# Early loads on one queue, position tables begun ahead, and a re-cut end of the last product and norm

## The chip, the cores and the metric

The kernel runs on one core of one Trainium2 chip. The metric is device time in microseconds (us) of one execution, from launch to the last output byte. Engines are named as the profile names them: PE (TensorE matrix products), PEld (its weight loads), DVE (VectorE), ACT (ScalarE), POOL (GpSimd) and SP (SyncE, used here to issue DMAs). Each engine works through its own instructions in order; engines wait for each other and for DMAs by semaphores.

## The reference

A decoder trunk of four pre-norm residual layers over one sequence of 256 tokens, width 1024, float32:

```python
cos, sin = rope_tables(positions)
h = x
for i in range(4):
    a = rms_norm(h, attn_norm_g[i])
    y = (diff_attention, moba_attention, swa_sink_attention)[i % 3](a, ...)   # w_in, heads, w_out
    h = h + y
    a = rms_norm(h, mlp_norm_g[i])
    h = h + square(maximum(a @ w_up[i], 0)) @ w_down[i]
return rms_norm(h, final_norm_g)
```

`rope_tables` turns the 256 integer positions into 8 cosines and 8 sines each, used by every mixer on the first 16 of each head's 64 dimensions. The differential attention of layers 0 and 3 also needs a number lambda from four short vectors. All weights, 183 + 2 pieces of 1 MB, are read from memory once.

## The kernel before

**Layout.** The residual stream lies transposed in four tiles `hT[j]`, each with two blocks `d` of 128 features by 256 tokens. Float32 products are made from three passes of a rounded format: each operand is split into a high and a low part, and `mm3` (lines 275 to 277) adds hi·hi, hi·lo and lo·hi in PSUM. A matmul of 128 x 128 by 128 x 512 is the unit.

**Weights.** `fetch` loads 1 MB pieces with DMAs issued from SP, into 4 buffers `raw`. `stage` rounds a piece on ACT into `whi` (line 80) and takes the rest on DVE into `wlo` (line 81), with 3 buffers of each. `take` hands out a piece, fetching 5 ahead and staging 2 ahead.

**Start.** Before any product there are: loads of `x` (by `load_x`: the first two blocks, the gains `gn` and the positions `posi` from ACT, the rest from SP between the pieces of the first two weight tiles, which come in quarters of 256 KB); 10 warm-up products on a tile of ones (20 PE instructions, line 134); staging of two pieces; and `norm_part` for each block `d`, which makes the high part of gain times `x` on ACT (line 232, tile `hg`) and the low part on DVE (line 233). `norm_sum` squares and adds (lines 237 to 246); `norm_factor` ends in `rsqrt`, whose result `nr` is applied when a product leaves PSUM.

**First layer.** `mixer_layer` makes six products `p_in` by `proj`, in the order q/k 0, q/k 1, v, q/k 2, q/k 3, v. After the first it emits `rotary_tables` (lines 156 to 192: some 37 DVE instructions of 16 elements in a chain, then two Sin on ACT, which need a table load) and `lambdas` (lines 195 to 206: a load `lv` from SP, DVE work, an Exp with its table load). `rope` (lines 306 to 311) then turns q and k, and the step `QK` transposes them on PE (`p_qk`, line 461).

**Order.** The code is written in the order of priority. A planner, which has its own estimate of times, sets the order in which each engine gets its instructions; that order is fixed when the program is built. PE too: in the trace `p_qk` stands behind 104 products `p_in`, though the code has it after 72.

**End.** `down_out` makes the last product, `p_last`, for two column halves `c` of 512 and two token halves `t` of 128. Eight weight pieces `q` with four blocks `k` each go into each half `c`. Each `c` ends with an update of the residual `res` on DVE (line 705), a sum of squares on ACT (line 707), and after the second half, for each `t`, the final norm: lines 712 and 713, `rsqrt` with 1 + 3 x 3 instructions on one column, a scaling of one half on ACT (line 716) and of the other on DVE (line 718), and two output DMAs.

Of the kernel before, what the change touches and what calls it, by code (L numbers as in the profile page):

```python
# [18 lines left out]
P = 128  # L19
D = 1024  # L20
# [9 lines left out]
FAR = 5  # L30
WARM = 10
RAW = 4
# [6 lines left out]
@with_exitstack  # L39
def trunk(ctx: ExitStack, tc: tile.TileContext, xT, positions, gains, lams, swa_row, fng, weights, out):  # L40
    nc = tc.nc
# [16 lines left out]

    def fetch(between=None):
        i = len(fetched)  # L60
        raw = sb.tile([P, 2048], F32, tag="raw", name=f"raw{i}", bufs=RAW)
        if between is None:
            nc.sync.dma_start(raw, weights[i])
        else:
            for h in range(4):
                s = slice(h * 512, (h + 1) * 512)
                nc.sync.dma_start(raw[:, s], weights[i, :, s])
                if h % 2:
                    between()
        fetched.append(raw)  # L70

    def stage():
        i = len(staged)
        raw = fetched[i]
        hi = sb.tile([P, 2048], F32R, tag="whi", name=f"whi{i}", bufs=LOOK + 1)
        lo = sb.tile([P, 2048], F32R, tag="wlo", name=f"wlo{i}", bufs=LOOK + 1)
        w = 512 if i < 2 else 1024
        for h in range(2048 // w):
            s = slice(h * w, (h + 1) * w)
            A.activation(hi[:, s], raw[:, s], AF.Copy)  # L80
            V.tensor_tensor(lo[:, s], raw[:, s], f(hi[:, s]), op=OP.subtract)  # L81
        staged.append((hi, lo))
# [12 lines left out]
    def r3(n):  # L95
        return lambda t: t.rearrange("p (a b) -> p a b", a=n)
# [3 lines left out]
    xv = xT.rearrange("(b p) t -> p b t", p=P)  # L100
    gn = cst.tile([P, 2 * DEPTH * 8 + 2], F32, name="gn")
    gv = gn[:, :2 * DEPTH * 8].rearrange("p (k l b) -> p k l b", k=2, l=DEPTH)
    posi = cst.tile([P, NT], I32, name="posi")
    loaded = []

    def load_x():
        j = len(loaded)
        if j == 0:
            nc.scalar.dma_start(hT[0][:, :S], xv[:, 0, :])
            nc.scalar.dma_start(gn, gains)  # L110
            nc.scalar.dma_start(hT[0][:, S:], xv[:, 1, :])
            nc.scalar.dma_start(posi, positions)
        elif j < 4:
            nc.sync.dma_start(r3(2)(hT[j]), xv[:, 2 * j:2 * j + 2, :])
        loaded.append(j)

    first_act = cst.tile([P, 1], F32, name="first_act")
    V.memset(first_act, 0.0)
    load_x()
# [8 lines left out]
    make_identity(nc, ident)  # L128
    ones = cst.tile([P, P], F32, name="ones")
    G.memset(ones, 1.0)  # L130

    warm = bank("wk", "p_warm")
# [18 lines left out]
    nlam = cst.tile([P, 2], F32, name="nlam")  # L151
    sg = gn[:, 2 * DEPTH * 8:]

    def rotary_tables():

        posf = cst.tile([P, NT], F32, name="posf")
        V.tensor_copy(posf, posi)
        inv = np.float32(THETA) ** (-np.arange(0, 16, 2, dtype=np.float32) / np.float32(16))
        invt = cst.tile([P, NT, 8], F32, name="invt")
        for j in range(8):  # L160
            G.memset(invt[:, :, j:j + 1], float(inv[j]))
        an = cst.tile([P, NT, 8], F32, name="an")
# [45 lines left out]
    def rsqrt(y, x, n):  # L208

        t = tiny.tile([P, n], F32, tag="nw", name="nw", bufs=5)  # L210
# [68 lines left out]
    def proj(n, widths, ahead=False, midway=()):  # L279
# [10 lines left out]
        steps = [(t, k) for t in range(NT) for k in range(8)]  # L290
        for t, k in sorted(steps, key=lambda x: x[1]) if ahead else steps:
            if (t, k) == (1, 0):
                for do in midway:
                    do()
            hi, lo = (r3(kb)(x)[:, k % kb, :] for x in parts[k // kb])
            s = slice(P * t, P * t + P)
            x = n.both[k // 2][:, k % 2]
            mm3(out[t], x[:, 0, s], x[:, 1, s], hi, lo,
                k == 0 and (t == 0 or width == 512 or not ahead), k == 7, skip_group_check=True)
        return out  # L300
# [179 lines left out]
    def mixer_layer(i, n):  # L480
# [46 lines left out]
        else:  # L527
# [32 lines left out]
            def OUT(g):  # L560
                if mixer == 0:
                    parts.extend(next(pairs[g]))

            order = (0, 1, "v", 2, 3, "v")
            plan = [[], [], [(QK, 0), (SC, 0)], [(SC, 1)], [(TR, 0), (QK, 1), (SC, 2)], [(TR, 1), (SC, 3)],
                    [(TR, 2), (AV, 0)], [(TR, 3), (AV, 1)], [(AV, 2), (QK, 2), (OUT, 0), (SC, 4)], [(AV, 3), (SC, 5)],
                    [(TR, 4), (QK, 3), (OUT, 1), (SC, 6)], [(TR, 5), (SC, 7)],
                    [(AV, 4), (TR, 6), (AV, 5), (TR, 7), (AV, 6), (OUT, 2), (AV, 7), (OUT, 3)]]
# [117 lines left out]
    def down_out(us, res, factor):  # L686

        grow = sb.tile([P, D], F32, tag="raw", name="grow", bufs=RAW)
        nc.sync.dma_start(grow, bcast(fng, D))
        ss = cst.tile([P, 2, NT], F32, name="fss")  # L690
        x = cst.tile([P, NT], F32, name="fx")
        r = cst.tile([P, NT], F32, name="fr")
        for c in range(2):
            cols = slice(512 * c, 512 * c + 512)
            banks = [bank("acc", "p_last") for _ in range(NT)]
            for q in range(8):
                hi, lo = (r3(4)(x) for x in take())
                steps = [(k, t) for k in range(4) for t in range(NT)]
                for k, t in steps if q < 7 else sorted(steps, key=lambda x: x[1]):
                    u, s = us[4 * q + k], slice(P * t, P * t + P)  # L700
                    mm3(banks[t], u[:, 0, s], u[:, 1, s], hi[:, k], lo[:, k], q + k == 0, q + k == 10,
                        skip_group_check=True)
            for t in range(NT):
                y = res[t][:, cols]
                V.scalar_tensor_tensor(y, banks[t], factor[:, t:t + 1], y, op0=OP.mult, op1=OP.add)
                sq = sb.tile([P, 512], F32, tag="relu", name="sq")
                A.activation(sq, y, AF.Square, accum_out=ss[:, c, t:t + 1])
                if c == 0:
                    V.tensor_tensor(y, y, grow[:, cols], op=OP.mult)
        for t in range(NT):  # L710
            o = slice(t, t + 1)
            V.tensor_tensor(x[:, o], ss[:, 0, o], ss[:, 1, o], op=OP.add)
            V.tensor_scalar(x[:, o], x[:, o], 1.0 / D, EPS, op0=OP.mult, op1=OP.add)
            rsqrt(r[:, o], x[:, o], 1)
            rows = slice(P * t, P * t + P)
            A.activation(res[t][:, :512], res[t][:, :512], AF.Copy, scale=r[:, o])
            nc.scalar.dma_start(out[rows, :512], res[t][:, :512])
            V.scalar_tensor_tensor(res[t][:, 512:], res[t][:, 512:], r[:, o], grow[:, 512:], op0=OP.mult, op1=OP.mult)
            nc.sync.dma_start(out[rows, 512:], res[t][:, 512:])

    n = new_norm(gv[:, 0, 0, :])
    for d in range(8):
        norm_part(n, d)
    for j in range(4):
# [111 lines left out]
```

## Time and profile before

| | us |
|---|---|
| median of 3 runs (lowest, highest) | 1159.29 (1159.09, 1159.89) |
| the profiled execution, its device time | 1158.97 |
| its span, first to last instruction | 1157.0 |
| busy: PE, PEld | 1139.8, 987.2 |
| busy: DVE, ACT, POOL | 822.5, 671.0, 11.4 |
| mean granted clock of PE | 0.995 |

The 1.97 us between device time and span lie outside the instructions. Busy PE time is counted from the start of a matmul to its modelled end; matmuls overlap, so a stream of them with no idle time can still run at two speeds, which the granted clock tells. A row of the timeline reads: start, duration, engine, line, operation, tiles, and in brackets the idle time of the engine before it with what ended it.

### The profile page before, as it was taken

The numbers are of one execution on the slowest core, as the hardware profiler recorded it, in microseconds if no ns is written. First come the engines' busy times: TensorE is split into PE (matmuls) and PEld (weight loads), VectorE is DVE, ScalarE is ACT, GpSimd is POOL, SyncE is SP. The second block draws the span as 40 slices with busy tenths as digits, with TensorE's granted clock in tenths as the row PEclk, the third lists the DMA queues.
The fourth block names the chain that finished last, engine by engine and source line by source line (L and its number), as shares of the span: only waits on it lengthen the run. The fifth ranks groups of instructions, "written<-read, shape, count | busy, mean of one in ns | idle before, by whom it ended". The sixth has DMA issues, their size and how long they took to land.

```text
span 1157.0 us, 17066 instructions
## 1 busy us (share of the span) xinstructions
PE 1139.8 (99%) x6544; PEld 987.2 (85%) x6544; DVE 822.5 (71%) x1632; ACT 671.0 (58%) x1237; POOL 11.4 (1%) x39
## 2 busy tenths in 40 slices
PE   8999999999999999999999999999999999999996
PEld 7788988888887888888899888888888889888885
DVE  7887877756676698766568787775567788777453
ACT  6776665544476775554446866654447676655341
POOL 1000000000000000000000000000000000000000
PEclk9999999999999999999999999999999999999998
DMA  8534465555543355555554245555553444554540
GB/s 309 192 132 144 146 218 183 183 193 197 193 136 125 136 187 184 190 205 186 182 206 140 80 146 198 202 183 184 186 202 129 154 148 143 194 191 164 194 170 36
DMA packets 30128, 198.65 MB, mean 172 GB/s; under 512 B 3552, under 2 KB 4704, under 8 KB 6624
## 3 DMA queue, kind: packets, MB, share of 16 engines
q1 hardware_dynamic: 29184, 196.76, 49.3%
q8 instruction: 51, 0.84, 0.3%
q10 hardware_dynamic: 864, 0.82, 0.2%
q14 instruction: 29, 0.24, 0.1%
HBM read 196.52 MB, written 1.05 MB: 171 GB/s over the span
## 4 chain that ended last, share of the span: by engine, by line
PE 92%; DVE 4%; ACT 2%; issue 1%; DMA 0%; ACTq 0%
PE p_up L598 20%; PE p_down L598 15%; PE p_up L599 11%; PE p_down L599 8%; PE p_in L277 6%; PE p_in L275 6%; PE p_in L276 6%; PE p_last L276 2%; PE p_last L275 2%; PE p_last L277 2%; DVE wlo L81 1%; PE p_t L353 1%; PE p_d L277 1%; PE p_d L275 1%; PE p_d L276 1%; PE p_av L436 1%
## 5 line engine op out<-in xcount | busy, mean ns | idle before, releaser
L81 DVE TENSOR_TENSOR wlo<-raw,whi 128x1024 fp32r<-128x1024 f32 (+1 forms) x374 | 446.9, 1209 | 198.4 <-ACT whi L80 198.2
L80 ACT ACTIVATE whi<-raw 128x1024 fp32r<-128x1024 f32 (+1 forms) x374 | 384.1, 1045 | 200.9 <-issue 103.5
L598 PE MATMUL p_up<-hg,whi 128*128 128x512 f32 x1024 | 356.7, 393 | 0.5 <-DVE hg L233 0.2
L599 PE MATMUL p_up<-hg,wlo 128*128 128x256 f32 x1024 | 285.5, 280 | 0.0
L598 PE MATMUL p_down<-uu,whi 128*128 128x512 f32 x768 | 266.4, 391 | 0.0
L598 PEld LDWEIGHTS p_up<-hg,whi 128*128 128x128 f32 x1024 | 191.4, 187 | 42.8 <-DVE hg L233 0.7
L599 PE MATMUL p_down<-uu,wlo 128*128 128x256 f32 x768 | 215.0, 280 | 0.0
L599 PEld LDWEIGHTS p_up<-hg,wlo 128*128 128x128 f32 x1024 | 193.5, 189 | 0.5
L598 PEld LDWEIGHTS p_down<-uu,whi 128*128 128x128 f32 x768 | 143.6, 187 | 31.5
L599 PEld LDWEIGHTS p_down<-uu,wlo 128*128 128x128 f32 x768 | 145.2, 189 | 0.0
L275 PE MATMUL p_in<-whi,hg 128*128 128x512 f32 (+1 forms) x368 | 137.9, 375 | 1.2 <-ACT hg L232 1.2
L276 PE MATMUL p_in<-wlo,hg 128*128 128x512 f32 (+1 forms) x368 | 135.7, 369 | 1.2 <-DVE wlo L81 1.2
L277 PE MATMUL p_in<-whi,hg 128*128 128x512 f32 (+1 forms) x368 | 136.7, 372 | 0.0
L671 ACT ACTIVATE uu<-u 128x512 fp32r<-128x512 f32 x64 | 40.5, 633 | 71.4 <-DVE u L669 69.9
L275 PEld LDWEIGHTS p_in<-whi,hg 128*128 128x128 f32 x368 | 69.8, 190 | 13.1 <-ACT hg L232 1.7
L276 PEld LDWEIGHTS p_in<-wlo,hg 128*128 128x128 f32 x368 | 69.7, 190 | 12.3 <-DVE wlo L81 1.5
L277 PEld LDWEIGHTS p_in<-whi,hg 128*128 128x128 f32 x368 | 69.6, 189 | 12.3 <-issue 0.5
L604 ACT ACTIVATE cross<-p_up 128x256 f32<-128x256 f32 x128 | 47.9, 374 | 39.3 <-PE p_up L599 33.8
L232 ACT ACTIVATE hg<-hT,gn 128x256 fp32r<-128x256 f32 x64 | 31.3, 503 | 65.5 <-DVE hT L617 65.3
L338 ACT ACTIVATE e<-ns,nm 128x128 f32<-128x128 f32 (+1 forms) x128 | 56.8, 446 | 10.5 <-DVE nm L335 10.4
L672 DVE TENSOR_TENSOR uu<-u,uu 128x512 fp32r<-128x512 f32 x64 | 44.2, 691 | 21.7 <-ACT uu L671 21.7
L275 PE MATMUL p_d<-oo,whi 128*128 128x256 f32 x192 | 55.6, 290 | 0.0
(184 smaller groups left out, 1364.9 us busy)
## 6 DMA issues: line engine op xcount, KB each, us to landing
raw<-in_weights SPq DMA_DIRECT2D x183, 1024.0 KB, 4.9
raw<-in_weights SPq DMA_DIRECT2D x8, 256.0 KB, 5.3
hT<-in_xT SPq DMA_DIRECT2D x3, 256.0 KB, 5.5
bias<-in_swa_row SPq DMA_DIRECT2D x1, 512.0 KB, 3.8
grow<-in_fng SPq DMA_DIRECT2D x1, 512.0 KB, 3.7
out<-res ACTq DMA_DIRECT2D x2, 256.0 KB, 2.9
out<-res SPq DMA_DIRECT2D x2, 256.0 KB, 2.6
hT<-in_xT ACTq DMA_DIRECT2D x2, 128.0 KB, 4.9
```

Of the source, the lines that this page charges most:

```text
L80: A.activation(hi[:, s], raw[:, s], AF.Copy)
L81: V.tensor_tensor(lo[:, s], raw[:, s], f(hi[:, s]), op=OP.subtract)
L232: A.activation(both[:, 0], h, AF.Copy, scale=g)
L275: T.matmul(out, lh, rh, start=start, stop=False, **kw)
L276: T.matmul(out, lh, rl, start=False, stop=False, **kw)
L277: T.matmul(out, ll, rh, start=False, stop=stop, **kw)
L338: A.activation(e[:, s], ns[:, s], AF.Exp, bias=nm[:, t:t + 1], scale=-1.0, accum_out=l[:, t:t + 1])
L598: T.matmul(r3(2)(p), hi, x, start=start, stop=False, skip_group_check=True)
L599: T.matmul(p[:, :S], lo, x[:, 0], start=False, stop=stop, skip_group_check=True)
L604: A.activation(cross, p[:, S:], AF.Copy)
L671: A.activation(both[:, :, 0], r3(2)(u), AF.Copy)
L672: V.tensor_tensor(both[:, :, 1], r3(2)(u), f(both[:, :, 0]), op=OP.subtract)
```

## The change

Five things are done together.

1. The positions travel as two more columns of `gains`, so one DMA brings both; it is the first on SP. No load is issued from ACT. SP then issues quarter by quarter: 256 KB of weights, then one block of `x` (128 KB), eight times; then the third and fourth weight pieces in halves. That is 21 DMAs.
2. `norm_part` of block `d` is emitted right before the staging of quarter `d` instead of after the staging of both pieces.
3. `rotary_tables` becomes a generator. Its first part (8 DVE instructions) is emitted ahead of the first staging, the rest where the whole was before. The constants `invt` and the ones are set on POOL ahead of the identity. `lambdas` moves from after the first product to between the step `QK` and the first scores, inside the second product. There are 11 warm-up products for 10.
4. In `proj`, where the input norm has only just been made (`ahead`), the passes of a block run as hi·hi for both `t`, then low part of `x`, then low part of the weights.
5. In the last product the pieces 6 and 7 are run for `t = 0` first, then for `t = 1`. In the second half `c`, the norm of `t = 0` is emitted in between; the last piece of `t = 1` is run in two column halves of 256, each closed by itself (`close`). The final norm (`finish`) takes 8 instructions of one column, and DVE scales its half in two pieces with an output DMA each.

```diff
-WARM = 10
+WARM = 11
-        w = 512 if i < 2 else 1024
         for h in range(2048 // w):
+            if first:
+                first()
     def load_x():
-            nc.scalar.dma_start(hT[0][:, :S], xv[:, 0, :])
-            nc.scalar.dma_start(gn, gains)
...
+        d = len(loaded)
+        nc.sync.dma_start(hT[d // 2][:, S * (d % 2):S * (d % 2) + S], xv[:, d, :])
+        loaded.append(d)
...
-    fetch(load_x)
-    fetch(load_x)
-    stage()
-    stage()
+    nc.sync.dma_start(gn, gains)
+    fetch(4, load_x)
+    fetch(4, load_x)
+    fetch(2)
+    fetch(2)
@@ rotary_tables, after the first three of its multiply-adds
+            if bits == 10:
+                yield
@@ proj
+        if ahead:
+            steps = [(t, k, x, w) for k in range(8) for x, w in ((0, 0), (1, 0), (0, 1)) for t in range(NT)]
@@ mixer_layer
-            plan = [[], [], [(QK, 0), (SC, 0)], [(SC, 1)], ...
+            plan = [[], [], [(QK, 0), (LAM, 0), (SC, 0)], [(SC, 1)], ...
-                    rotary_tables()
-                    lambdas()
+                    next(tables, None)
@@ down_out
+        def close(t, bank, c, part, first, width):
+            y = res[t][:, 512 * c + first:512 * c + first + width]
+            V.scalar_tensor_tensor(y, bank[:, first:first + width], factor[:, t:t + 1], y, op0=OP.mult, op1=OP.add)
+            sq = sb.tile([P, 512], F32, tag="relu", name="sq")
+            A.activation(sq[:, :width], y, AF.Square, accum_out=ss[:, part, t:t + 1])
+        def finish(t, halves):
+            V.scalar_tensor_tensor(last, ss[:, halves, o], 0.5 / D, x[:, 0, o], op0=OP.mult, op1=OP.add)
+            V.tensor_scalar(y.bitcast(I32), last.bitcast(I32), -0.5, 1597463007.0 - 2.0 ** 22 - 2.0 ** 31, ...)
+            for _ in range(3):
+                V.scalar_tensor_tensor(w, y, y, last, op0=OP.mult, op1=OP.mult)
+                V.scalar_tensor_tensor(y, w, 1.5, y, op0=OP.subtract, op1=OP.mult)
+            A.activation(res[t][:, :512], res[t][:, :512], AF.Copy, scale=y)
+            nc.scalar.dma_start(out[rows, :512], res[t][:, :512])
+            for z in (slice(512, 768), slice(768, 1024)):
+                V.scalar_tensor_tensor(res[t][:, z], res[t][:, z], y, grow[:, z], op0=OP.mult, op1=OP.mult)
+                nc.sync.dma_start(out[rows, z], res[t][:, z])
...
+            ends = [(q, k) for q in (6, 7) for k in range(4)]
+            last(0, ends)
+            close(0, banks[0], c, c, 0, 512)
...
+                finish(0, 1)
+                last(1, ends[:4])
+                for h in range(2):
+                    last(1, ends[4:], slice(256 * h, 256 * h + 256))
+                    close(1, banks[1], 1, 1 + h, 256 * h, 256)
+                    if h == 0:
+                        sofar(1, [1])
+                finish(1, 2)
@@ start of the work
+    tables = rotary_tables()
+    next(tables)
     n = new_norm(gv[:, 0, 0, :])
+    blocks = iter(range(8))
+    for _ in range(2):
+        stage(512, lambda: norm_part(n, next(blocks)))
```

More of the change, by code (lines that the diff above doesn't have):

```diff
@@ L39, in trunk @@
 @with_exitstack
-def trunk(ctx: ExitStack, tc: tile.TileContext, xT, positions, gains, lams, swa_row, fng, weights, out):
+def trunk(ctx: ExitStack, tc: tile.TileContext, xT, gains, lams, swa_row, fng, weights, out):
     nc = tc.nc
@@ L57, in trunk, with fetch, stage @@
     fetched, staged = [], []
-    def fetch(between=None):
+    def fetch(parts=1, along=None):
         i = len(fetched)
         raw = sb.tile([P, 2048], F32, tag="raw", name=f"raw{i}", bufs=RAW)
[L62 to L69, printed above, removed]
+        w = 2048 // parts
+        for h in range(parts):
+            s = slice(h * w, (h + 1) * w)
+            nc.sync.dma_start(raw[:, s], weights[i, :, s])
+            if along:
+                along()
         fetched.append(raw)
-    def stage():
+    def stage(w=1024, first=None):
         i = len(staged)
@@ L157, in rotary_tables @@
         V.tensor_copy(posf, posi)
[L158 to L161, printed above, removed]
         an = cst.tile([P, NT, 8], F32, name="an")
@@ L693, in down_out, with sofar @@
+        def sofar(t, parts):
+            o = slice(t, t + 1)
+            V.tensor_scalar(x[:, 0, o], ss[:, 0, o], 0.5 / D, 0.5 * EPS, op0=OP.mult, op1=OP.add)
+            for j in parts:
+                V.scalar_tensor_tensor(x[:, 0, o], ss[:, j, o], 0.5 / D, x[:, 0, o], op0=OP.mult, op1=OP.add)
         for c in range(2):
-            cols = slice(512 * c, 512 * c + 512)
             banks = [bank("acc", "p_last") for _ in range(NT)]
-            for q in range(8):
[L697 to L719, printed above, removed]
+            parts = []
@@ new lines, in down_out @@
+            ends = [(q, k) for q in (6, 7) for k in range(4)]
+            last(0, ends)
+            close(0, banks[0], c, c, 0, 512)
+            if c == 0:
+                last(1, ends)
+                close(1, banks[1], 0, 0, 0, 512)
+                for t in range(NT):
+                    y = res[t][:, :512]
+                    V.tensor_tensor(y, y, grow[:, :512], op=OP.mult)
+                    sofar(t, [])
+            else:
+                finish(0, 1)
[6 more added lines that the diff above has]
+                finish(1, 2)
```

68 lines of the change are left out of this document (40 added, 28 removed).

## The prediction

> **What bounds the kernel now.** I read the page first (engine shares, chain), then busy time by stages, then the waits of PE, then the timeline at both ends.
>
> The page's engine row and the stretches (times, then busy us of PE, PEld, DVE, ACT, POOL; granted clock; DMA share; GB/s):
>
> ```profile
> PE 1139.8 (99%) x6544; PEld 987.2 (85%) x6544; DVE 822.5 (71%) x1632; ACT 671.0 (58%) x1237; POOL 11.4 (1%) x39
> ```
> ```profile
> 5.00:10.00 5.00, 2.60 (x9) 1.51 (x9) 2.40 (x7) 3.24 (x7) 0.87 (x11) 0.98 0.91 255
> 10.00:13.43 3.43, 3.43 (x10) 2.61 (x10) 3.43 (x8) 3.15 (x8) 0.00 (x0) 0.53 1.02 362
> 13.43:34.52 21.09, 21.09 (x96) 17.30 (x94) 18.75 (x67) 15.78 (x24) 0.00 (x0) 1.00 0.92 356
> 36.00:1147.60 1111.60, 1108.53 (x6416) 961.82 (x6416) 791.54 (x1527) 643.79 (x1195) 6.25 (x12) 1.00 0.49 168
> ```
>
> PE is the bound: from 36 to 1147.6 us it idles 3.1 us in 1111.6. The change adds and removes no matmul there, except twelve that are halved. So it can win or lose only in the first 36 us, where PE waits and for 3.43 us runs at clock 0.53, and in the 9.4 us after the last product. The longest wait of PE from 20 us to that point, in total, times, longest:
>
> ```profile
> PE p_o L411 <- DVE o L406: 2.4, 6, 0.5
> ```
>
> These belong to the attention of layers 0 and 3 and stay. The next one, 1.3 at `p_qk`, is where the rotary tables are late.
>
> **The start, product side.** PE, the SP queue's waits in the first 8 us, DVE and ACT:
>
> ```profile
> 1.14 4.64 PE L134 MATMUL p_warm<-ones 128*128 128x128 f32 x20 [1.14 <-POOL ones L130]
> 6.94 0.50 PE L275 MATMUL p_in<-whi,hg 128*128 128x512 f32 x1 [1.16 <-ACT hg L232]
> 8.64 0.50 PE L276 MATMUL p_in<-wlo,hg 128*128 128x512 f32 x1 [1.20 <-DVE wlo L81]
> ```
> ```profile
> SPq L67 <- DMA hT<-in_xT: 2.6, 1, 2.6
> ```
> ```profile
> 7.81 0.17 DVE L157 CAST posf<-posi 128x2 f32<-128x2 int32 x1 [1.53 <-DMA posi<-in_positions]
> 7.90 0.69 DVE L81 TENSOR_TENSOR wlo<-raw,whi 128x512 fp32r<-128x512 f32 x1
> ```
> ```profile
> 9.11 0.48 DVE L233 SCALAR_TENSOR_TENSOR hg<-hT,gn,hg 128x256 fp32r<-128x256 f32 x1
> ```
> ```profile
> 5.02 0.63 ACT L80 ACTIVATE whi<-raw 128x512 fp32r<-128x512 f32 x1 [0.87 <-DMA raw<-in_weights]
> ```
> ```profile
> 6.39 0.49 ACT L232 ACTIVATE hg<-hT,gn 128x256 fp32r<-128x256 f32 x1
> ```
>
> `whi` is there at 5.65, yet its `wlo` starts at 7.90: DVE stands in `posf`, waiting for the positions, the last load of the ACT queue. SP lost 2.6 us on a wait of a weight load for the landing of the first `x` block, eight loads before it; I read that as eight loads in flight at most. What follows from PE's 2.4 us of idling is the slow clock from 10.0 to 13.4.
>
> How much PE loses: three rows for all `p_in` ahead of `p_qk`, and the price of a matmul from the chain, where L598 and L599 have 1024 each.
>
> ```profile
> L276 PE MATMUL p_in<-wlo,hg 128*128 128x512 f32 x35 | 14.3, 408 | 1.2 <-DVE wlo L81 1.2
> L275 PE MATMUL p_in<-whi,hg 128*128 128x512 f32 x35 | 14.3, 408 | 1.2 <-ACT hg L232 1.2
> L277 PE MATMUL p_in<-whi,hg 128*128 128x512 f32 x34 | 14.1, 420 | 0.0
> ```
> ```profile
> PE p_up L598 20%; PE p_down L598 15%; PE p_up L599 11%; PE p_down L599 8%; PE p_in L277 6%; PE p_in L275 6%; PE p_in L276 6%; PE p_last L276 2%; PE p_last L275 2%; PE p_last L277 2%; DVE wlo L81 1%; PE p_t L353 1%; PE p_d L277 1%; PE p_d L275 1%; PE p_d L276 1%; PE p_av L436 1%
> ```
>
> 20% of 1157 over 1024 is 0.226 us for 512 columns; 11% gives 0.124 for 256. The 104 products are 23.5 us; the 96 in 21.09 us of the stretch above agree (0.22). With the four small `p_sum` among them, put at 0.124 each, a dense stream lasts 24.0 us. It ended at 34.5, so it was worth a start at 10.5, though the first product ran at 6.94.
>
> After the change: gains and positions come first and nothing of ACT competes. The first quarter was staged at 5.02 with another queue's loads mixed in; it is now issued one DMA later (0.43, the `lv` row below) but alone. I take 4.3 to 5.0 for `whi`, half a microsecond more for the `x` block, and 5.5 for the first `hg`. PE is still in its warm-ups then: they start some 0.1 earlier and are 22 x 0.232 = 5.1 us, so they end at 6.1. From there I expect a dense stream. A block `k` is 6 x 0.226 = 1.36 us on PE, 0.63 + 0.49 = 1.12 on ACT and 0.69 + 0.48 = 1.17 on DVE, so both engines keep ahead. The 384 KB of a block are 1.09 us at the 362 GB/s of 10 to 13.4, but 1.54 at the 255 of 5 to 10. All at the low rate, the eighth `hg` would come at 5.5 + 7 x 1.54 = 16.3, where PE wants it at 6.1 + 7 x 1.36 = 15.6: 0.7 late. With the third piece behind it, I bound the loss by supply at 0 to 1.4 and take 0.5, nearer the row of 362, since SP now keeps its eight loads filled. No idle time before means no stretch of half clock.
>
> So PE reaches `p_qk` at 6.1 + 24.0 = 30.1.
>
> **The start, table side.** ACT, DVE and PE around the stall:
>
> ```profile
> 30.23 2.01 ACT L80 ACTIVATE whi<-raw 128x1024 fp32r<-128x1024 f32 x2 [1.50 <-issue]
> 32.26 1.28 ACT L189 ACT_TABLE_LOAD   x1
> 33.56 0.22 ACT L189 ACTIVATE sn<-an 128x16 f32<-128x16 f32 x1
> ```
> ```profile
> 34.37 0.42 DVE L199 TENSOR_TENSOR lp<-lv 128x256 f32<-128x256 f32 x1
> 34.71 0.42 DVE L306 TENSOR_TENSOR ropea<-qk,cc 128x256 f32<-128x256 f32 x1
> 35.04 0.41 DVE L201 TENSOR_REDUCE ls<-lp 128x4 f32<-128x256 f32 x1
> 35.37 0.42 DVE L311 TENSOR_TENSOR qk<-ropea,ropeb 128x256 f32<-128x256 f32 x1
> ```
> ```profile
> 34.29 0.39 PE L276 MATMUL p_in<-wlo,hg 128*128 128x512 f32 x1
> 35.93 0.30 PE L461 MATMUL p_qk<-ident,qk 128*128 128x128 f32 x1 [1.25 <-DVE qk L311]
> ```
>
> The Sin and its table load stand on ACT behind two `whi`, which waited for PE to free a buffer. `lp` and `ls` of lambda take 0.67 us (two steps of 0.33) right in the rope that PE waits for. Two ways to the new time: if the Sin stays behind those `whi`, it moves with PE, 4.4 earlier, and lambda's 0.67 is gone: 35.93 - 5.1 = 30.8. If DVE's queue sets it: DVE starts on weights at about 5.0 for 7.9 (2.9 earlier), eight table steps, at the 0.193 of the small steps of the end, are done before (1.5), lambda 0.67: 30.9. I take 30.9, a stall of 0.8; bounds 0 (the Sin goes ahead of the `whi`) and 1.9 (none of the eight steps pays). Front: 35.93 - 30.9 = 5.0, less 0.5 for supply, is 4.5. Free by cover: the eight early steps lie before the first weights; if gains land late, each 0.2 delays `wlo`. The re-ordered passes of `proj` and the eleventh warm-up (0.46) lie under the wait for data.
>
> `lv` is the one load that moves back: its issue stands on SP behind one more pair of weight pieces, each of which waits for a buffer.
>
> ```profile
> 23.26 0.43 SPq L197 DMA_DIRECT2D lv<-in_lams  x1
> 25.58 4.08 SPq L63 DMA_DIRECT2D raw<-in_weights  x2
> ```
> ```profile
> DMA to landing us min/median/max: 4.6/4.9/10.7
> ```
>
> (The last row is that of all 183 later weight loads.) It goes from 23.3 to behind the second of those two, which was issued at 29.3, 24.5 in the new time. It lands 5 to 6 later, at 30, before lambda's work, which now follows `p_qk`. Price 0, or what rival 4 says.
>
> **The end.** The last product, DVE, ACT:
>
> ```profile
> 1147.28 0.39 PE L277 MATMUL p_last<-whi,uu 128*128 128x512 f32 x1
> ```
> ```profile
> 1147.95 0.74 DVE L705 SCALAR_TENSOR_TENSOR res<-p_last,factor,res 128x512 f32<-128x512 f32 x1
> ```
> ```profile
> 1148.73 0.63 ACT L707 ACTIVATE sq<-res 128x512 f32<-128x512 f32 x1 [2.23 <-DVE res L705]
> ```
> ```profile
> 1150.05 0.15 DVE L712 TENSOR_TENSOR fx<-fss 128x1 f32<-128x1 f32 x1
> ```
> ```profile
> 1152.36 0.75 DVE L718 SCALAR_TENSOR_TENSOR res<-res,fr,grow 128x512 f32<-128x512 f32 x1
> ```
>
> From the last matmul's start to the end of `res` are 5.83 us. The twelve small steps from 1150.05 to 1152.36 are 0.193 each. DVE was also in the way of itself: L705 waited for the other half's chain, L712 for its scaling. With pieces 6 and 7 run for `t = 0` first, that half is closed 5.7 us before PE ends, and its chain (0.74 + 0.63 + 0.14 + 1.5 + 0.75 = 3.8) is over when `t = 1` needs DVE.
>
> The split of the last piece costs PE: 24 x 0.124 - 12 x 0.226 = 0.27. And the second column half writes a PSUM bank that DVE is just reading for the first. What that does, `p_d` shows, whose blocks share banks by halves too:
>
> ```profile
> 123.49 0.28 PE L277 MATMUL p_d<-oo,wlo 128*128 128x256 f32 x1
> ```
> ```profile
> 123.76 1.08 DVE L617 TENSOR_TENSOR hT<-p_d,hT 128x256 f32<-128x256 f32 x3
> ```
> ```profile
> 124.94 0.28 PE L275 MATMUL p_d<-oo,whi 128*128 128x256 f32 x1
> ```
>
> The other halves come only after DVE has read, 0.10 after its end, and PE did products `p_up` in between. Here nothing is left to do in between: 0.27 + 0.42 + 0.10 - 0.12 = 0.67 us of stall, bounds 0 and 0.9. The Trainium skill, PSUM — Partial Sum Buffer, section "PSUM bank collisions raise a hardware error", speaks against this edit in the same sense: two engines may not use one bank at once, even at different addresses, so software must separate them. By it the stall is there; by address alone it would be 0.
>
> ```profile
> L604 ACT ACTIVATE cross<-p_up 128x256 f32<-128x256 f32 x128 | 47.9, 374 | 39.3 <-PE p_up L599 33.8
> ```
>
> New end: last matmul at 1147.28 + 0.23 + 0.94 - 0.12 = 1148.33; DVE 0.27 later, 0.42; the square of 256 columns 0.37 (this row; 0.63 for 512) and, as I estimate, 0.14 to hand over: 1149.53. Eight steps of 0.193: 1151.07. Two scalings of 256: 0.75, 1151.8 for 1153.1. The end gains 1.3; as the last DMA waits its turn on SP (0.43) I take 1.2, bounds 0.5 and 1.9 (no bank stall).
>
> **Sum.** 4.5 + 1.2 = 5.7. From the profiled 1158.97 (span 1157.0 and 1.97 around it) that is 1153.3; the median of the runs is 0.3 above the profiled one, so 1153.6.
>
> **Rivals.** (1) Supply: small loads stay at 255 GB/s, PE starves and one stretch at 0.53 comes back: 1.4 + 1.6 of the front's 5.0 are lost, and 2.0 + 1.2 gained: 1156.1. For it: DMA was 0.91 busy at that low rate. The Trainium skill, DMA: Bandwidth & Descriptors, "Rules for kernel authors", asks for 1 MiB per DMA; the change goes the other way. Against: 362 GB/s in 10 to 13.4, with quarters too. 12%. (2) The tables come no earlier than 2 us, as the planner puts the rest of the chain as late as before: `p_qk` at 33.9, end 0.5: 1156.8. 10%. (3) Better: no stall at `p_qk`, no bank stall: 5.8 + 1.9, 1151.6. 6%. (4) Slower: `lv` lands late. DVE is in order, so `lp` blocks weights and scores behind it, and PE with them. With the worst landing, 10.7, and its issue not moved (29.7), `lv` lands at 40.4; lambda's place is about 31.5. 8.9 of stall against 5.7: 1162.5. It decides from a landing after 37. Against it: the median landing of 4.9. 7%. (5) The planner's order undoes the early parts, no change: 1159. 3%.
>
> **Numbers.** The forecast has 62%. Its own range is 1152.2 to 1156; rivals (1) and (2) lie at 1156.1 and 1156.8, so 1152.2 to 1157.2 leaves out (3), (4), (5) and some ends of the others. 0.2% (2.3 us) is what a measurement can tell from none. Faster: the forecast, (1), (3) and part of (2): 0.83; same: 0.09; slower: 0.08.
>
> **What would show it.** `p_in` dense from 6.1 with no stretch below clock 1.0 until the end; no DVE wait for positions; `p_qk` near 31; PE idle about 0.7 between the two column halves; eight steps of 0.19 before the last scalings. Wrong would be: `hg` or `wlo` waits of PE after 7 us, `p_qk` after 33, DVE waiting for `lv`.

## The result and the profile after

The changed kernel takes 1155.47 us (median of 6 runs, 1154.68 to 1155.63), the kernel before, run beside it, 1159.48 (6 runs, 1158.85 to 1159.89). The ratio is 0.9966, 95% interval 0.9955 to 0.9976: 4.0 us are won, where 5.7 were forecast. The profiled execution took 1155.61 us, its span is 1153.7 where it was 1157.0, so the two profiles to be compared stand 3.3 us apart.

Busy time by stretch, in the columns of the prediction's first fence; the last row is the kernel before:

```profile
5.00:10.00 5.00, 5.00 (x21) 3.55 (x21) 3.72 (x7) 4.37 (x10) 0.94 (x2) 1.00 0.94 302
10.00:13.43 3.43, 3.43 (x17) 2.77 (x16) 3.43 (x9) 3.43 (x8) 0.00 (x0) 1.00 0.98 330
13.43:20.00 6.57, 5.85 (x27) 4.39 (x26) 5.53 (x17) 4.15 (x7) 0.00 (x0) 1.00 0.99 359
```
```profile
13.43:20.00 6.57, 6.57 (x30) 5.41 (x29) 6.24 (x20) 5.73 (x11) 0.00 (x0) 1.00 1.02 427
```

PE now idles nowhere between 5 and 13.43 us and the clock of 0.53 is gone. What is new is the third row: 0.72 us of idling where the kernel before had none, with the DMA engines 99% busy but 359 GB/s moved where it was 427. The waits of PE (total, times, longest) and one of SP's queue in the first 60 us:

```profile
PE p_o L409 <- DVE o L404: 2.4, 6, 0.5
PE p_qk L459 <- DVE qk L309: 0.7, 1, 0.7
PE p_s L271 <- issue: 0.6, 1, 0.6
PE p_last L271 <- DVE res L698: 0.6, 1, 0.6
PE p_in L296 <- DVE wlo L81: 0.5, 1, 0.5
```
```profile
SPq L66 <- DMA raw<-in_weights: 5.0, 6, 2.7
```

The first is the old one of the attention. The wait at `p_qk` (1.3 before) and the one at `p_last`, the column halves, were forecast. Those at `p_in` and `p_s` were not; waits of PE for `wlo` after 7 us are one of the prediction's signs of being wrong. The timeline of PE and ACT at the third weight piece:

```profile
5.71 0.75 PE L296 MATMUL p_in<-whi,hg 128*128 128x512 f32 x2
...
18.23 0.73 PE L296 MATMUL p_in<-whi,hg 128*128 128x512 f32 x2 [0.20 <-ACT whi L80]
19.49 0.50 PE L296 MATMUL p_in<-wlo,hg 128*128 128x512 f32 x1 [0.53 <-DVE wlo L81]
```
```profile
17.12 1.06 ACT L80 ACTIVATE whi<-raw 128x1024 fp32r<-128x1024 f32 x1 [1.91 <-DMA raw<-in_weights]
18.41 1.06 ACT L80 ACTIVATE whi<-raw 128x1024 fp32r<-128x1024 f32 x1 [0.24 <-DMA raw<-in_weights]
```

The first `p_in` starts at 5.71 (6.94 before), in time; but ACT then stands 1.91 us in front of a weight piece that has not landed. The other new wait, at the first scores, on ACT and PE:

```profile
33.90 2.01 ACT L80 ACTIVATE whi<-raw 128x1024 fp32r<-128x1024 f32 x2
35.93 0.59 ACT L475 ACTIVATE kpadh<-p_qk 64x512 fp32r<-64x512 f32 x1
```
```profile
36.62 0.59 PE L271 MATMUL p_s<-kpadh,qhl 128*128 128x256 f32 x2 [0.60 <-issue]
```

The label "issue" hides the cause: PE starts when the keys' second half (`kpadh`, started at 35.93) is made, and that stands on ACT behind two `whi`.

The end, DVE, PE and ACT:

```profile
1144.28 0.48 DVE L698 SCALAR_TENSOR_TENSOR res<-p_last,factor,res 128x256 f32<-128x256 f32 x1
1147.61 0.16 DVE L706 SCALAR_TENSOR_TENSOR fx<-fss,fx 128x1 f32<-128x1 f32 x1 [0.58 <-ACT sq L700]
1149.34 0.88 DVE L718 SCALAR_TENSOR_TENSOR res<-res,fr,grow 128x256 f32<-128x256 f32 x2
```
```profile
1144.82 0.39 PE L271 MATMUL p_last<-whi,uu 128*128 128x256 f32 x1 [0.58 <-DVE res L698]
```
```profile
1147.07 0.42 ACT L700 ACTIVATE sq<-res 128x256 f32<-128x256 f32 x1 [1.76 <-DVE res L698]
```

PE stands between the two column halves while DVE reads the bank, and resumes 0.06 after DVE's end at 1144.76.

**A ledger of PE.** The table sums, for each trace, what the distance of successive product starts exceeds the usual one (0.226 us for a `p_in`), from the first `p_in` to the first `p_o`, by place; times in us. Small losses elsewhere are left out.

| | before | changed | whole pieces | whole, `wlo` first | tables late | pairs of x | pairs, unsplit |
|---|---|---|---|---|---|---|---|
| first `p_in` | 6.94 | 5.71 | 5.72 | 5.72 | 5.71 | 6.00 | 6.00 |
| lost to 13.2 | 3.5 | 0.8 | 1.1 | 1.1 | 1.0 | 0.8 | 1.4 |
| lost 13.2 to 23.8 (third piece) | 0.1 | 1.7 | 2.4 | 1.1 | 0.9 | 0.1 | 0.2 |
| lost at `p_qk` | 1.4 | 0.8 | 0.1 | 0.6 | 1.3 | 0.8 | 0.8 |
| lost at the first `p_s` | 0.0 | 0.8 | 0.3 | 0.2 | 0.3 | 0.8 | 0.8 |
| `p_in` ahead of `p_qk` | 104 | 98 | 90 | 116 | 112 | 96 | 96 |
| first `p_o` | 71.6 | 69.1 | 69.0 | 68.1 | 68.5 | 67.6 | 68.3 |

The start is not the same in every execution: three other profiles with the changed kernel's start (the front alone, the unsplit end, the padded one, below) lost 0.7, 0.9 and 1.9 at the third piece. A difference of less than 1 us in one place of one profile says nothing by itself.

### The profile page after: what moved, and what is told of

Same layout as the page of the kernel before. It is cut to its first block, busy times and chain, and to the rows that moved or that the text cites. A ratio compares the mean times of both kernels' runs of the same rounds, so it can differ in the third digit from the quotient of the medians.

```text
span 1153.7 us, 17107 instructions
## 1 busy us (share of the span) xinstructions
PE 1140.0 (99%) x6558; PEld 987.4 (86%) x6558; DVE 824.2 (71%) x1631; ACT 672.1 (58%) x1239; POOL 11.5 (1%) x39
## 4 chain that ended last, share of the span: by engine, by line
PE 92%; DVE 5%; DMA 1%; ACT 1%; issue 1%; SPq 0%; DVEq 0%; ACTq 0%
PE p_up L599 20%; PE p_in L296 16%; PE p_down L599 15%; PE p_up L600 11%; PE p_down L600 8%; PE p_last L271 2%; PE p_last L273 2%; PE p_last L272 2%; DVE wlo L81 2%; PE p_t L351 1%; PE p_d L273 1%; PE p_d L271 1%; PE p_d L272 1%; PE p_av L434 1%; PE p_s L271 1%; DMA raw<-in_weights 1%
## 5 line engine op out<-in xcount | busy, mean ns | idle before, releaser
L296 PE MATMUL p_in<-whi,hg 128*128 128x512 f32 (+1 forms) x736 | 213.2, 372 | 0.2 <-ACT whi L80 0.2
L599 PEld LDWEIGHTS p_down<-uu,whi 128*128 128x128 f32 x768 | 143.6, 187 | 31.5
L296 PEld LDWEIGHTS p_in<-whi,hg 128*128 128x128 f32 x736 | 132.0, 189 | 24.3 <-issue 1.2
L296 PE MATMUL p_in<-wlo,hg 128*128 128x512 f32 (+1 forms) x368 | 130.3, 368 | 0.5 <-DVE wlo L81 0.5
L228 ACT ACTIVATE hg<-hT,gn 128x256 fp32r<-128x256 f32 x64 | 31.7, 504 | 65.4 <-DVE hT L618 65.2
L271 PE MATMUL p_d<-oo,whi 128*128 128x256 f32 x192 | 55.7, 290 | 0.0
L272 PE MATMUL p_d<-oo,whi 128*128 128x256 f32 x192 | 54.7, 285 | 0.0
L606 DVE TENSOR_TENSOR relu<-p_up,cross 128x256 f32<-128x256 f32 x128 | 53.6, 419 | 1.6 <-ACT cross L605 1.2
```

Of the source, the lines that this page charges most:

```text
L271: T.matmul(out, lh, rh, start=start, stop=False, **kw)
L272: T.matmul(out, lh, rl, start=False, stop=False, **kw)
L296: T.matmul(out[t], n.both[k // 2][:, k % 2, x, P * t:P * t + P], r3(kb)(parts[k // kb][w])[:, k % kb, :], start=fresh, stop=k == 7 and x + ...
L599: T.matmul(r3(2)(p), hi, x, start=start, stop=False, skip_group_check=True)
L606: V.tensor_tensor(out, p[:, :S], cross, op=OP.add)
```

## The experiments

Medians and ratios are to the kernel before, run beside each; half the width of an interval is about 1 us, so that variants of the changed kernel are told apart by their traces, and by medians only where the runs do not overlap.

**The end alone.** The kernel before with the new `down_out`.

> The kernel before with the new last product and final norm alone; the front as before. Theory (the two parts add up, the end is worth 1.2 us as the trace has it from the last matmul's neighbourhood on: 9.72 us before, 8.55 us after): 1.2 us faster than before, 1158.1 to 1158.5, with the 0.6 to 0.9 us wait of PE at p_last behind DVE's read of the bank present. Rival (the front's earlier work shifts the end, the end alone is worth 0.3 or nothing): within 0.5 us of before.

Measured: 1157.65 us, ratio 0.9991 (0.9982 to 0.9999), 1.3 below the 1158.96 beside it.

**The front alone.** The changed kernel with the old `down_out`.

> The changed kernel with the old last product and final norm. Theory: what is left of the front's gain at the last product, 2.1 us by the offset of the two traces' matmuls there: 1157.0 to 1157.6 beside 1159.4 for before, and 1.2 us slower than the changed kernel. Rival (front and end share a cost, as a DMA or an engine that both touch): the sum of this gain and that of the end alone differs from the 4.0 us measured for both by more than 1 us.

Measured: 1156.39 us, ratio 0.9976 (0.9966 to 0.9985), 2.6 below the 1158.96, a little more than the 1.8 to 2.4 that the expectation gave it. 1.3 and 2.6 make 3.9, as both together (4.0): within what these runs tell, the two parts are independent, and the end is worth what it was forecast. What is missing is the front's.

**The last piece not split.**

```diff
-                last(1, ends[:4])
-                for h in range(2):
-                    last(1, ends[4:], slice(256 * h, 256 * h + 256))
-                    close(1, banks[1], 1, 1 + h, 256 * h, 256)
...
-                finish(1, 2)
+                last(1, ends)
+                close(1, banks[1], 1, 1, 0, 512)
+                finish(1, 1)
```

> The changed kernel with the last piece of the second token tile in full width and closed once (no column halves, one close of 512, seven small steps behind it as before). Theory (the halves cost PE 0.74 us for the wait on the bank and some 0.27 us for narrow matmuls, and save one 512-wide DVE close and its Square, 0.75 - 0.48 and about 0.26, so that the split loses): 0.2 to 0.6 us faster than the changed kernel. Rival (the wait of PE costs nothing because something else, the first tile's scalings, would hold DVE there anyway): 0.4 to 0.6 us slower.

Measured: 1154.79 us (1154.22 to 1155.73), ratio 0.9964 (0.9951 to 0.9976). Last product on PE, then DVE:

```profile
1144.24 0.39 PE L273 MATMUL p_last<-whi,uu 128*128 128x512 f32 x1
```
```profile
1144.67 0.75 DVE L698 SCALAR_TENSOR_TENSOR res<-p_last,factor,res 128x512 f32<-128x512 f32 x1 [1.28 <-PE p_last L273]
1146.21 0.16 DVE L706 SCALAR_TENSOR_TENSOR fx<-fss,fx 128x1 f32<-128x1 f32 x1 [0.79 <-ACT sq L700]
```

From the first `p_last` to the end of the span are 94.93 us here, 95.43 in the changed kernel, 96.55 before. So the halves lose 0.5: they shorten the tail behind the last product by less than PE's wait and the narrow products cost. By the traces the theory holds; the medians lie 0.7 apart, but the runs overlap.

**Third and fourth piece whole.** `fetch()` for `fetch(2)`, twice.

> The changed kernel with the third and fourth weight piece loaded whole, in rows of 8 KB, not in two halves of 4 KB rows. Theory (between 13 and 17 us packets of 4 KB move only 127 to 180 KB in half a us where the whole pieces of before moved 210 to 237, and that is what made the third piece late): PE's gaps at 17.8 and 18.8 us (0.68 and 0.92) shrink by half or more, the first product's end comes 0.5 to 1.2 us earlier, and the time falls by 0.4 to 1.2 us. Rival (the bytes ahead of the piece and the wait for earlier landings decide, not the packets): the same within 0.2 us, as a whole piece is complete only when its last row is.

Measured: 1155.71 us (1155.12 to 1157.46), ratio 0.9975 (0.9966 to 0.9984): no faster. ACT, DVE and PE:

```profile
16.80 2.01 ACT L80 ACTIVATE whi<-raw 128x1024 fp32r<-128x1024 f32 x2 [1.65 <-DMA raw<-in_weights]
```
```profile
18.11 0.16 DVE L251 TENSOR_SCALAR nx<-p_sum 128x2 f32<-128x2 f32 x1
...
19.50 1.22 DVE L81 TENSOR_TENSOR wlo<-raw,whi 128x1024 fp32r<-128x1024 f32 x1
```
```profile
20.77 0.50 PE L296 MATMUL p_in<-wlo,hg 128*128 128x512 f32 x1 [2.01 <-DVE wlo L81]
```

The whole piece is there at 16.80, when the changed kernel had not even its first half (17.12), as the theory wanted; the gap of PE grew nevertheless. `whi`'s first half is ready at 17.8, but the planner, whose order follows its own estimate of times, has put small steps of the norm and the tables ahead of `wlo` on DVE, until 19.5. Neither theory had that.

**Whole pieces, `wlo` first.** As before, with the third piece staged ahead of the norm, and the norm's and the tables' DVE steps held behind its `wlo`.

```diff
+    stage()
+    third = rest[0]
...
-        r = norm_factor(n)
+        with tc.issue_after(third.ins):
+            r = norm_factor(n)
...
-                    next(tables, None)
+                    with tc.issue_after(third.ins):
+                        next(tables, None)
```

> The third and fourth weight piece whole, as in the run before, and DVE's order held so that both wlo of the third piece stand ahead of the input norm's steps and of the rest of the tables. Theory (whole pieces do land earlier, the third complete at 16.8 where its second half came at 18.3 in the changed kernel, and only DVE's order, which put 12 to 18 small steps of norm and tables ahead of the first wlo, lost 2.0 us of PE there): PE's gap at the third piece falls from 2.39 us to 0.8 or less, and the time is 0.6 to 1.6 us below that of whole pieces alone, 1154.1 to 1155.1. Rival (what stands behind wlo on DVE then comes late and p_qk pays for it): the gap closes, but p_qk's stall grows by as much, and the time stays within 0.3 us of whole pieces alone.

Measured: 1155.08 us (1154.76 to 1155.31), ratio 0.9967 (0.9955 to 0.998), 0.6 below the run above, the lower end of what was expected. The wait:

```profile
PE p_in L296 <- DVE wlo L81: 0.5, 1, 0.5
```

Of the 1.3 us that came back at the third piece, 0.6 went to `p_qk`. Both theories have a part.

**Tables on POOL.** The chain's DVE steps as POOL steps (a multiply-add as two), the last three on DVE, DVE's and the Sin held behind the third piece, which is staged early as above.

```diff
-            V.tensor_scalar(q, an, 1.0 / turn, None, op0=OP.mult)
+            G.tensor_scalar(q, an, 1.0 / turn, None, op0=OP.mult)
...
-                V.scalar_tensor_tensor(x, q, -c, x, op0=OP.mult, op1=OP.add)
+                G.tensor_scalar(w, q, -c, None, op0=OP.mult)
+                G.tensor_tensor(x, w, x, op=OP.add)
```

> The changed kernel with the chain of the position tables on POOL (the multiply-adds as two steps each), its last three steps on DVE and the Sin behind the third piece. Theory (p_qk is set by the small steps of DVE behind the third piece, some 24 of the tables between 19.4 and 27.4 us; POOL idles): the angles are there by 20 us, rope follows the norm factor at once, the 0.7 us stall at p_qk goes, the scores start earlier, and the time falls by 0.6 to 1.5 us. Rival (p_qk is set by PE's own stream and the loads of weights, the stall only moves to the next wait): the time stays within 0.3 us of the changed kernel. POOL's steps do not show in any trace so far; at over 0.5 us a step the angles come after 28 us and it would be slower.

Measured: 1169.16 us, ratio 1.0089 (1.0076 to 1.0103): 10.3 us slower than before. Two steps on POOL, then DVE:

```profile
18.69 1.08 POOL L179 TENSOR_TENSOR an<-an,turns 128x16 f32<-128x16 f32 x1
...
22.81 0.23 POOL L172 TENSOR_TENSOR an<-step,an 128x16 f32<-128x16 f32 x1
```
```profile
18.45 1.24 DVE L81 TENSOR_TENSOR wlo<-raw,whi 128x1024 fp32r<-128x1024 f32 x1
...
25.31 0.17 DVE L184 TENSOR_SCALAR an<-an 128x16 f32<-128x16 f32 x1 [3.93 <-POOL an L182]
```

A step of this kind that takes POOL 0.23 us while DVE idles takes 1.08 while DVE makes a `wlo`. The angles come at 25.3 instead of 20, and DVE, in order, waits 3.93 us for them with `wlo` queued behind; PE with it (4.0 us between two products). The test of the tables is spoilt by that. The Trainium skill, GPSIMD Engine Reference, section "8. Key points", says that POOL shares its memory interfaces with DVE and gets in conflict with DVE instructions of two inputs in SBUF; `wlo` is one, and the trace agrees. The front explains 4.2 us of the loss against the changed kernel, a stretch of half clock behind PE's wait among them (28.5 to 31.9, shown with the longer warm-up below); the rest is in the chapter on the hardware.

**Lambda's work back** at its old place: `(LAM, 0)` out of the plan, `lambdas()` behind `next(tables, None)`.

> The changed kernel with lambda's work back behind the first product, ahead of QK. Theory (its two steps of 0.33 on DVE stood in the rope that PE waited for at p_qk; the prediction gave them 0.67): p_qk 0.5 to 1.5 us later by the trace, the time 0.3 to 0.9 us above the changed kernel. Rival (there is other work to do for PE, or the new wait at p_s, 0.6 us, came from moving it): within 0.2 us of the changed kernel, or up to 0.5 us faster, with no wait at p_s.

Measured: 1155.48 us (1155.18 to 1155.74), ratio 0.997 (0.9959 to 0.9981), as the changed kernel. `p_qk` comes 3.3 us later, with 113 `p_in` ahead of it; PE loses 1.5 there and 0.25 at `p_s`, together about as much as in the changed kernel (0.8 and 0.8). Moving lambda shows no gain.

**Tables wholly late.** All steps of the chain held behind the last low part of the input on DVE.

```diff
-    next(tables)
...
-                    next(tables, None)
+                    with tc.issue_after(n.end.ins):
+                        for _ in tables:
+                            pass
```

> The changed kernel with every step of the tables held behind the last low part of the input on DVE (16.0 us), so none of the chain runs early. Theory (the chain of small steps behind the third piece sets p_qk; 13 of its steps of 0.21 us come in addition there, 2.7 us): p_qk 2 to 4 us later, of which PE can fill a part with products of later pieces; time 1.0 to 2.5 us above the changed kernel. The prediction's step put the early part at 1.5. Rival (the supply of weights is the limit and p_qk's place is free): within 0.3 us.

Measured: 1154.46 us (1154.39 to 1155.26), ratio 0.9964 (0.9951 to 0.9976): not slower. PE:

```profile
34.69 1.06 PE L459 MATMUL p_qk<-ident,qk 128*128 128x128 f32 x8 [1.09 <-DVE qk L309]
```

`p_qk` does come 2.9 us later than the changed kernel's 31.75, and that costs nothing, since the planner lays 112 instead of 98 `p_in` ahead of it. My theory falls: `p_qk` may come this much later at no cost, and the early start of the tables shows no gain.

**The kernel before, warmed longer.** `WARM = 17` for 10.

> The kernel before with 17 warm-up products for 10 and nothing else; they then end near 9.0 us, where the first real product came at 6.94. Theory (in the first 13.45 us PE lost 3.5 us after its first real product, of which some 1.7 are the stretch at half clock, and that stretch follows from PE's idling between 5.8 and 8.6 us): with no idling there is no half clock; real products start 2 us later and still reach the 104th earlier, by 0.5 to 1.5 us, but the tables then hold p_qk, so that 0 to 1.2 us of it reach the end: 1157.7 to 1159.0, clock 1.00 from the start on. Rival (the half clock has another cause, as the time since the start): the stretch is there as before and the time is 1 to 2 us longer.

Measured: 1158.22 us (1158.0 to 1159.11), ratio 0.9992 (0.9983 to 1.0001), 0.8 below the 1158.98 beside it. Its stretches, and its warm-ups:

```profile
5.00:10.00 5.00, 3.36 (x22) 2.69 (x22) 2.39 (x7) 3.28 (x7) 0.87 (x11) 1.00 0.92 271
10.00:13.43 3.43, 3.43 (x17) 2.82 (x16) 3.43 (x8) 3.43 (x9) 0.00 (x0) 1.00 0.94 308
```
```profile
1.14 6.11 PE L134 MATMUL p_warm<-ones 128*128 128x128 f32 x34 [1.14 <-POOL ones L130]
```

The clock is 1.00 in the stretch that had 0.53, with the same loads and nearly the same first `p_in` (7.02 for 6.94). In this execution the half clock is gone with PE's idling, 2.40 us between 5 and 10 before against 1.64 here, and so it does not follow from the time since the start. The run with the tables on POOL agrees: the clock is halved behind PE's wait of 3.64 us. Its stretch, and that of the kernel before, taken from change to change of the clock:

```profile
28.48:31.88 3.40, 3.40 (x10) 2.26 (x9) 1.94 (x7) 2.45 (x4) 0.00 (x0) 0.50 0.51 154
```
```profile
9.78:13.19 3.41, 3.41 (x9) 2.63 (x10) 3.41 (x8) 3.13 (x8) 0.00 (x0) 0.50 1.01 352
```

The Trainium skill, TensorE: Matmul & The Clock Gate, section "What's actually happening", describes a clock that is halved until PE has been busy for about 3.4 us; the two stretches at 0.50 were as long. It is not so in every execution: in the trace of the end alone, which has the start of the kernel before, the half clock lasts 6.8 us, from 7.75 to 14.57, with 0.6 us of idling in it.

What the half clock costs by itself stays open. The one execution with a trace is the slowest of the eleven, 1159.11, and its first `p_o` comes at 71.63 where it was 71.62: PE lost the gain again to waits (1.2 us at `p_sum`). The 0.8 us of the medians lie in runs without a trace, and the interval reaches 1.

**x in pairs.** Two blocks of x in one load with rows of 2 KB, for which the host lays x out in pairs, the second weight piece in halves: 15 loads for 21 (the 13 of the expectation is a miscount).

```diff
-        nc.sync.dma_start(hT[d // 2][:, S * (d % 2):S * (d % 2) + S], xv[:, d, :])
+        nc.sync.dma_start(hT[j], xT[j])
...
-    fetch(4, load_x)
+    fetch(2, load_x)
```

> The changed kernel with x laid out so that two blocks come in one load of 256 KB with rows of 2 KB, and the second weight piece in halves: 13 loads for 21 ahead of the fifth piece, the order of need kept. Theory (the changed kernel lost 2.5 us by supply, 0.84 until 13.45 and 1.66 at the third piece, or 1.5 to 1.8 in all in other profiles of the same start, because 1 and 2 KB rows move 260 to 340 KB in a us where whole pieces move 430): the third piece lands 0.5 to 1.2 us earlier and PE loses 0.5 to 1.2 us less, 1154.3 to 1155.0. Rival (the engine work on the first blocks, not the bytes, is the limit, and bigger loads come too coarse: the second block waits for its whole pair): the same within 0.3 us or up to 0.5 us slower.

Measured: 1154.65 us (1154.2 to 1155.46), ratio 0.9963 (0.995 to 0.9975). Stretches of the changed kernel, then of this one (last column GB/s), and its ACT:

```profile
9.00:11.00 2.00, 2.00 (x8) 1.34 (x8) 2.00 (x6) 2.00 (x5) 0.00 (x0) 1.00 0.98 341
13.00:15.00 2.00, 2.00 (x11) 1.65 (x10) 2.00 (x5) 2.00 (x5) 0.00 (x0) 1.00 0.99 301
```
```profile
9.00:11.00 2.00, 2.00 (x11) 1.65 (x10) 1.97 (x7) 1.75 (x4) 0.00 (x0) 1.00 1.02 390
13.00:15.00 2.00, 2.00 (x11) 1.62 (x10) 2.00 (x4) 2.00 (x6) 0.00 (x0) 1.00 1.03 422
```
```profile
14.77 4.03 ACT L80 ACTIVATE whi<-raw 128x1024 fp32r<-128x1024 f32 x4
```

ACT stages the third and fourth piece without any wait, from 14.77 where it was 17.12, and PE's loss there goes from 1.7 (0.7 to 1.9) to 0.1. Supply was the limit. It is not a matter of 4 KB rows, as I had thought: the same half pieces in rows of 4 KB move at 422 GB/s here and at 301 there. Whether the longer rows of x or the smaller number of loads did it was not tried apart, and the time alone does not show the gain: the intervals of the two ratios all but coincide.

**A pad of 32 bytes**, with the unsplit end:

```diff
+    pad = cst.tile([P, 8], F32, name="pad")
+    G.memset(pad, 0.0)
```

> The changed kernel with the last piece of the second token tile in full width, and one unused tile of 32 bytes a partition ahead of the working tiles, so that every tile that PE reads starts at a multiple of 128 bytes (96 over one before). In the run with the tables on POOL a new tile of 64 bytes moved the same tiles to 32 over a multiple of 128, and a third of the products p_down and p_up were 6 to 8% longer, some 9 us in all. Theory (the start address of what PE reads decides): a change of the pace of p_down and p_up, in either direction, by up to 9 us; at 128 exactly most likely no slower than now. Rival (POOL's late work or other tiles did it): the pace of products is as before, 224 and 112 ns, and the time is that of the unsplit end, 1154.8.

Measured: 1154.25 us (1154.06 to 1155.38), ratio 0.996 (0.9948 to 0.9973): the pace of products is that of the unsplit run, and so is the time, within what the runs tell. The rival holds.

**Pairs and the unsplit end together.**

> The two edits that paid, together on the changed kernel: x in pairs with fewer, longer loads, and the last piece of the second token tile in full width. Theory (the front's supply loss and the end's bank wait are independent; the pairs took 1.6 us of PE's loss at the third piece away and the full width 0.5 us at the end): the third piece costs PE 0.1, no wait between column halves, span near 1151.6, time 1153.6 to 1154.4, some 1 to 1.8 us below the changed kernel. Rival (the 0.8 us of gain in pairs came from one lucky execution of the loads): 1154.8, as the unsplit end alone.

Measured: 1154.0 us (1153.77 to 1154.33), ratio 0.9954 (0.9941 to 0.9968). It is the fastest version: all its five runs lie below the lowest of the changed kernel's six, 1154.68, 1.5 us by medians, though the two were not run beside each other and the intervals of the ratios overlap. The third piece costs 0.2; 0.6 of what was expected beyond went to the first blocks (1.4 lost to 13.2).

## Why the prediction was right, and where not

The direction and the range held, and so did the mechanism of the end and of the start's first 8 us. The time came out 1.9 us above the forecast (1153.6 forecast, 1155.47 measured) and the gain 1.7 below it, all of it in the front: supply cost more than its bound, and what the front was to win by earlier tables shows in no run. One of the prediction's own signs of being wrong came: PE waits for `whi` and `wlo` after 7 us (0.20 and 0.53). A first product 0.4 us earlier than forecast and 0.4 in small gains, neither worked out beforehand, made up for a part.

- **The end: 1.2 forecast, 1.12 in the profile (95.43 us for 96.55), 1.3 by the run of the end alone.** The stall was put at 0.67: the last product before it starts at 1143.96 and the next at 1144.82, 0.86 for the usual 0.12, so 0.74. DVE is out of its own way (1147.61 waits for ACT alone). The eight steps take 1.73 us, not 8 x 0.193, since the three with a tensor as their scalar take 0.25 each from start to start; the scalings 0.88, not 0.75.
- **No half clock, dense from 6.1:** 1.00 throughout, and no idling from 5.71 to the third piece. The 22 warm-ups end before 6.1 since their starts are 0.213 apart, not 0.232.
- **Supply, 0.5 taken with bounds of 0 to 1.4: the step that failed.** The ledger has 2.5 us (0.8 to 13.2, 1.7 at the third piece), 1.5 to 2.7 over the four profiles of this start: past the bound. I took the best stretch of before, 362 GB/s, as the nearer end for the whole of the fill; it went at 302, 330 and, where the third piece came, 301. I costed the eight blocks by it but not the third piece, which I had named and which has no slack behind them. And I took SP's eight loads in flight to be enough; SP waited 5.0 us for landings. The pairs of x show it: with longer rows of x and fewer loads the third piece costs 0.1.
- **`p_qk` at 30.9 with a stall of 0.8: measured 31.75, 0.65.** The stall was right, but the measure was wrong. I counted the front's gain by the time of `p_qk`, taking 104 `p_in` ahead of it for granted. The planner laid 98, so 6 x 0.226 = 1.4 of the 4.2 us by which `p_qk` is earlier are work put off. By the first `p_o` the front is 2.5 ahead, 2.1 at the first `p_last`. (The 0.4 between are lost in layer 1, whose instructions the change leaves alone; the run of the end alone shows them against the profile of before as well.)
- **Lambda 0.67 and eight early steps 1.5: no gain shows.** Each was a true time on the way to `p_qk`, but PE had other products to do: with lambda back and with the tables late the time is no longer, within the 1 us or so that the runs tell.
- **Nothing was forecast at `p_s`;** 0.6 us of wait came there, since the keys' second half stands behind two `whi` on ACT.
- **The rivals.** The first came half true: PE did starve, though at the third piece and without the half clock. `lv` was never waited for, but not for the reason given: it was issued at 31.7, not 24.5, and landed some 5.9 later, beyond the 37 from which the fourth rival counted a loss. What saved it is the planner, which laid lambda's first step at 40.1 and not at 31.5.

In the ledger's terms I expected 0.8 (start) + 3.5 (to 13.2) + 0.6 (`p_qk`) less 0.5, which is 4.4, and got 1.2 + 2.7 + 0.6 - 1.6 - 0.8, with 0.4 more in small gains behind `p_qk`: 2.5.

## What to carry to other kernels

Count a gain on the engine that bounds the kernel by the time it no longer loses, not by when one instruction starts: where a planner can lay other work ahead, that instruction moves by microseconds at no cost, as `p_qk` did. Before cutting early loads into pieces, compare the rate that a fill of such loads reached in a trace with the rate that the consumer needs, and look at the first large load behind them, which paid here. A split that makes a writer wait for a reader of the same bank must save more than that wait, which was 0.74 us here for a read of 0.48.

## What the runs showed of the hardware that I had not expected

- Warm-up products double their pace on the way, and the profile's 1.00 hides it: in the longer warm-up their starts are 0.213 us apart until 5.35 and 0.111 from 5.52. The trace's records of the clock begin at 5.46 in that run, and where there is no record the profile shows 1.00. In the end alone the pace changes between 4.29 and 4.43 and the records begin at 4.33, in the pairs of x between 3.94 and 4.11 and at 4.06. Products `p_in` are 0.427 apart at 0.50 and 0.226 at 1.00, nearly the same ratio, so I take the first warm-ups to have run at half clock. The full clock came between 4.1 and 6.7 us in the traces of this case, so two executions need not start alike: in the front alone it came at 6.63, and the first two `p_in` stand 0.57 and 0.40 us before the next.
- Small POOL steps are stretched nearly five times by a DVE instruction beside them (0.23 and 1.08 us, above).
- With the tables on POOL the products `p_up` and `p_down` of the first three layers ran longer, in a steady pattern. The tile's instructions in the changed kernel, then in that one (count; ns at least, median, most):

```profile
L599 PE MATMUL p_down<-uu,whi x256: 391/391/391, 212.9 to 301.3; 128*128 128x512 f32 x128
```
```profile
L603 PE MATMUL p_down<-uu,whi x256: 395/398/403, 218.6 to 308.7; 128*128 128x512 f32 x128
```

That is 1.8% (173.4 against 176.6 ns from start to start, in the mean over both passes) and about 9 us over three layers. The `p_up` of the last layer ran at 391 again in the same execution, and moving all working tiles by 32 bytes changed nothing. The cause stays open; a move by 64 bytes, as in that run, was not tried by itself.
- The half pieces of 4 KB rows moved at 301 GB/s between 13 and 15 us in the changed kernel, at 422 in the run with pairs. Why the rate was low there, with the DMA engines 99% busy, stays open too.
